# Attention of a hybrid mixer on one core: the two heads of a pair on the halves of the tensor engine's array

## The chip, the core and the metric

The kernel runs on one core of a Trainium2 chip. A core has a tensor engine (TensorE, PE in the views; PEld is its weight load), VectorE (DVE), ScalarE (ACT), GpSimd (POOL) and SyncE (SP), which work from queues of their own and wait for each other by semaphores. SBUF holds operands in 128 partitions, PSUM takes the matmuls' results in banks of 512 f32 columns. A matmul keeps one operand in the array (the stationary one, loaded ahead) and streams the other through it (the moving one). The metric is the device time of one execution in microseconds (us), less is better.

## What is computed

Two layers over 512 tokens of width 1024. Each layer projects the tokens, runs three mixers side by side (dilated attention with 8 heads of 64, retention, gated linear attention), multiplies by gates and an output matrix, and adds a feed forward with a short convolution; layer norms follow both. The change is in the attention, whose three dilated branches the reference computes and then merges:

```
scores = jnp.einsum('bhrnqd,bhrnkd->bhrnqk', qb, kk).astype(jnp.float32) * (d ** -0.5)
...
p = jnp.exp(scores - m[..., None])
l = p.sum(-1)
o = jnp.einsum('bhrnqk,bhrnkd->bhrnqd', p, vv) / l[..., None]
...
ya = merge_heads(head_norm(dilated_attention(qa, ka, va)))
```

The kernel takes the three branches at once: with a common maximum they are one softmax in which a key counts as often as branches see it (constant `mult`; `neg` masks the others). Head norm makes the common denominator drop out but for its epsilon, so the sums of values are normed as they are, with a term from the denominators (`ll`).

## The kernel before, in words

Every large product is made of leading and remaining parts, three passes each in fp32r (`mm3`, L202 to L205): lead x lead, lead x rest, rest x lead. Weights are loaded by SyncE's queue in tiles of 512 KB (`weight_tile`, L180), ScalarE rounds the leading part (L189), VectorE subtracts it (L190). Plain f32 products run as two passes each in the records. A transpose is a matmul with the identity (L277).

Attention (L573 to L677): for each of two groups of four heads, `project_heads` (L574) projects, rotates and transposes queries and keys: a block holds two heads, one in partitions 0 to 63, the other in 64 to 127. Values are projected once (`vv`, L663). The group has two pairs of heads (u = 0, 1), so a layer has four pairs and the kernel eight. For a pair:

- `scores` (L591), once for each head. Query tile i (128 tokens) meets the keys 0 to (i+1)*128, at least 256 columns, in three groups: tile 3, tile 2, tiles 0 and 1. The operands lie in 64 partitions, so the matmul uses the half of the array's rows in which its head lies. Each group takes one PSUM bank (`bank()`, four in all) and one page of SBUF (tag "pg", nine in all). VectorE masks, scales and finds the maximum (L607), ScalarE takes the exponential (L610), VectorE multiplies by `mult` and sums (L611).
- `weighted` (L616): for each head and each group of key tiles ((0,), (1, 3), (2,)) the numerators are transposed, 128 x 128 at a time, into a bank, ScalarE copies them to a page (L636), and `products` (L622) multiplies. There a 128 x 128 block of transposed numerators is the stationary operand and 64 columns of values move (L626): 10 matmuls for each head, all of a pair into one bank, tokens in the partitions. The transposes of a group come ahead of the products of the one before it.
- `finish` (L643): ScalarE squares the sums (L323), VectorE reduces them (L325), takes a reciprocal root (L304 to L308) and scales (L331). `finish_rows` (L648) transposes the pair's block after the next pair's scores, or, for the last pair, in the middle of the output product.

The order of the instructions is not written out by hand: a scheduler takes, for each engine, the ready instruction of the lowest number, with numbers set by `at(...)`. In a layer: pairs of the first group 6000 and 6400, values 7000, second group's heads 8000, its pairs 9000 and 9400, gates 9200, output product 20000. So while a pair waits for its softmax, TensorE's queue has projections. The order is fixed when the kernel is built; at run time each engine takes its queue in order.

Two other places use halves of the array and are not changed: L499 (states of the gated linear attention) multiplies 64 partitions by 64 partitions, one half of the rows for each value of c, into two banks; L555 writes 64 partitions of one bank with 64 stationary columns, then the other 64 with other operands.

Of the kernel before, what the change touches and what calls it, by code (L numbers as in the profile page):

```python
# [13 lines left out]
AF = mybir.ActivationFunctionType  # L14
ALU = mybir.AluOpType
# [25 lines left out]
def weight_chunks():  # L41
    """One layer's weights: name -> tiles of (rows, columns), in the order of their use."""
    w = {}
# [30 lines left out]
def weight_offsets():  # L74
    """(layer, name) -> tiles of (offset in the packed weights, rows, columns per row)."""
    at, out = 0, {}
    for l in range(DEPTH):
        for name, tiles in weight_chunks().items():
            out[l, name] = []
            for ks, c in tiles:  # L80
                out[l, name].append((at, len(ks), width(c)))
                at += P * len(ks) * width(c)
    return out
# [57 lines left out]
def hymba(ctx: ExitStack, tc: tile.TileContext, x, xt, wpk, prm, wal, lnv, cst, out):  # L141
# [38 lines left out]
    def weight_tile(l, name, i, lo_engine, raw=None):  # L180
        """A tile of weights: for each of its row blocks the leading and the remaining part."""
        o, nk, w = offsets[l, name][i]
# [28 lines left out]

# [1 line left out]
    c_sb = cp.tile([P, NCONST], F32, tag="cst", name="cst")  # L213
# [9 lines left out]
    def load_xt(t, raw, loads=1, parts=1):  # L223
        """A tile of tokens, transposed, in two parts: loaded at once or in pieces, and taken apart in pieces."""
        pieces = lambda a: a.rearrange("p (k t) -> p k t", k=KD)
# [18 lines left out]
    def start():  # L244
        """The first chunk of weights and the tokens, the first to be used ahead of the others. Products of zeros
        bring the tensor engine's clock up while they are loaded."""
        idle = page("yrg")
# [39 lines left out]
    def rope(ps, nh, dim, cname, t, a):  # L287
        """Rotates nh heads of dim from PSUM into a page."""
        half = dim // 2
# [11 lines left out]
    def rsqrt(v, n, tag):  # L301
        """v ** -0.5: an estimate from the exponent, and two Newton steps."""
        r, t = small(n, tag), small(n, tag)
        V.tensor_scalar(r.bitcast(I32), v.bitcast(I32), -0.5, 0x5F376908, op0=ALU.mult, op1=ALU.add)  # L304
        for c in (1.5008789, 1.5000006):
            V.tensor_mul(t, r, r)
            V.scalar_tensor_tensor(out=t, in0=t, scalar=-0.5, in1=v, op0=ALU.mult, op1=ALU.mult)
            V.scalar_tensor_tensor(out=r, in0=t, scalar=c, in1=r, op0=ALU.add, op1=ALU.mult)  # L308
        return r

    def centred(ps, out, tag):
        """Values less their mean over each head, so that the heads' outputs have mean zero."""
        p3 = ps.rearrange("p (g d) -> p g d", d=64)
# [6 lines left out]
    def normed(ps, more, scale, tag, small_tag):  # L320
        """Eight groups of 64 with mean zero, over the root of (their sum of squares + more)."""
        sq = page(tag)
# [12 lines left out]
    def to_rows(ps, scale, tag):  # L335
        """A block of the mixer's output, transposed, times its scale, as two parts."""
        h = page(tag, 512, F32R)
# [5 lines left out]
    def norm_rows(t, gb, last_layer):  # L343
        """Layer norm of token tile t, and out of the chip after the last layer."""
        mv = small(2, "s_ln")
# [18 lines left out]
    def to_columns():  # L364
        """The first of the normalized token tiles that wait for it, transposed, in two parts."""
        if pending:
# [16 lines left out]
    def token_gemm(rows, kt, tail, done, between=None):  # L383
        """Four token tiles of a product of rows[k] (stationary) and kt[k]; done(ps, t) takes each."""
        n = len(kt)
# [19 lines left out]
    for l in range(DEPTH):  # L405
# [4 lines left out]
        base = l * 1000000  # L410
# [1 line left out]
        at(base + 1000)  # L412
# [33 lines left out]
        at(base + 2500)  # L446
        # log sigmoid, its sums within chunks, and their exponentials
        la = page("yrg")
# [24 lines left out]
        bm128 = bmask.unsqueeze(2).to_broadcast([P, HR, P])  # L473
# [1 line left out]
        at(base + 3000)  # L475
# [12 lines left out]
        at(base + 4000)  # L488
        # states of the gated linear attention before each chunk
        gstate = [None] * 9  # L490
        for t2 in range(2):
# [13 lines left out]
            for u in range(4 if t2 == 0 else 3):  # L505
# [5 lines left out]
                gstate[i + 1] = s_  # L511
        # retention and gated linear attention, one token tile after another
        ynat = []
# [58 lines left out]

# [1 line left out]
        def project_heads(g):  # L574
            """Queries and keys of four heads, rotated and transposed, in two parts: blocks of two heads."""
            qk = x4("qk", F32R)
# [13 lines left out]

        def scores(qk, low, u, hh, l3):  # L591
            """Softmax's numerators of one head of pair u in a group, by query tile; sums into l3."""
            hs = slice(hh * 64, hh * 64 + 64)
            probs = [None] * NT
            nmx = small(4, "s_at")
            for group in ((3,), (2,), (0, 1)):
                sc, pr, o = bank(), page(), 0
                for i in group:
                    n, m = (i + 1) * P, max(256, (i + 1) * P)
                    ts = slice(i * P, (i + 1) * P)  # L600
                    mm3(sc[:, o:o + m], qk[hs, u, ts], low[u][hs, ts], qk[hs, 2 + u, 0:m], low[2 + u][hs, 0:m], True, True)
                    probs[i] = (sc[:, o:o + n], pr[:, o:o + n])
                    o += m
                for i in group:
                    s_, p_ = probs[i]
                    m0 = (3 - i) * P
                    V.tensor_tensor_reduce(out=p_, in0=s_, in1=C("neg")[:, m0:], op0=ALU.add, op1=ALU.min,  # L607
                                           scale=-0.125, scalar=3e38, accum_out=nmx[:, i:i + 1])
                    with tc.issue_after(tables.ins):
                        A.activation(out=p_, in_=p_, func=AF.Exp, scale=-1.0, bias=nmx[:, i:i + 1])  # L610
                    V.tensor_tensor_reduce(out=p_, in0=p_, in1=C("mult")[:, m0:], op0=ALU.mult, op1=ALU.add,  # L611
                                           scale=1.0, scalar=0.0, accum_out=l3[:, i, hh:hh + 1])
                    probs[i] = (s_, p_)
            return [p_ for _, p_ in probs]

        def weighted(pr, c0, o4):  # L616
            """The two heads' sums of values, weighted, into o4: a group of key tiles is transposed ahead of the
            products of the one before it."""
            groups = [(hh, js) for hh in range(2) for js in ((0,), (1, 3), (2,))]
            ready = []  # L620

            def products(hh, js, pt):  # L622
                o = 0
                for j in js:
                    for i in range(j, NT):
                        mmul(o4[:, i, hh, :], pt[:, o:o + P], vv[:, j, c0 + hh * 64:c0 + hh * 64 + 64],  # L626
                             start=(hh == 0 and j == 0 and i == 0), stop=(hh == 1 and js == groups[-1][1] and i == NT - 1))
                        o += P

            for hh, js in groups:  # L630
                bk, pt, o = bank(), page(), 0
                for j in js:
                    for i in range(j, NT):
                        transpose(bk[:, o:o + P], pr[hh][i][:, j * P:(j + 1) * P])
                        o += P
                A.copy(pt[:, :o], bk[:, :o])  # L636
                ready.append((hh, js, pt))
                if len(ready) > 1:
                    products(*ready.pop(0))
            for r in ready:  # L640
                products(*r)

# [15 lines left out]
        for g in range(2):  # L658
# [8 lines left out]
            for u in range(2):  # L667
# [3 lines left out]
                l3 = ll.rearrange("p (i h) -> p i h", h=2)  # L671
                pr = [scores(qk, low, u, 0, l3)]
                finish_rows()
                pr.append(scores(qk, low, u, 1, l3))
                o = bank()
                o4 = o.rearrange("p (i h d) -> p i h d", i=4, h=2)
                weighted(pr, p2 * P, o4)  # L677
                finish(o, ll, p2)

# [1 line left out]
        at(base + 9200)  # L681
# [13 lines left out]

# [1 line left out]
        stats = [sp.tile([P, 12], F32, tag="stats", name=nm("st"), bufs=8) for _ in range(NT)]  # L697
# [23 lines left out]

# [1 line left out]
        def conv(ps, c):  # L723
# [100 lines left out]
```

## Time and profile before

| | |
|---|---|
| time, median of 3 runs | 1265.61 us (1265.24 to 1268.29) |
| span of the profiled execution, first to last instruction | 1262.7 us |
| instructions | 15680 |
| TensorE busy | 1246.5 us, 99% |
| VectorE busy | 786.7 us, 62% |
| ScalarE busy | 448.0 us, 35% |
| DMA moved | 116.05 MB, mean 92 GB/s |

The profile gives the profiled execution's own time as its span of 1262.7 us; the timed runs contain also what lies before the first and after the last instruction. A matmul's duration runs from its issue to the end of its way through the array, and the next one begins before that, so prices of TensorE's work are read from start to start. A busy share says that an engine had something under way, not that it was at its peak.

### The profile page before, as it was taken

The numbers are of one execution on the slowest core, as the hardware profiler recorded it, in microseconds if no ns is written. First come the engines' busy times: TensorE is split into PE (matmuls) and PEld (weight loads), VectorE is DVE, ScalarE is ACT, GpSimd is POOL, SyncE is SP. The second block draws the span as 40 slices with busy tenths as digits, with TensorE's granted clock in tenths as the row PEclk, the third lists the DMA queues.
The fourth block names the chain that finished last, engine by engine and source line by source line (L and its number), as shares of the span: only waits on it lengthen the run. The fifth ranks groups of instructions, "written<-read, shape, count | busy, mean of one in ns | idle before, by whom it ended". The sixth has DMA issues, their size and how long they took to land.

```text
span 1262.7 us, 15680 instructions
## 1 busy us (share of the span) xinstructions
PE 1246.5 (99%) x6180; PEld 1036.1 (82%) x6180; DVE 786.7 (62%) x1519; ACT 448.0 (35%) x621; POOL 16.6 (1%) x26
## 2 busy tenths in 40 slices
PE   9999999999999999999999999999999999999997
PEld 7777888898888888888887778888988888888885
DVE  5676676587664356664767757767776633566646
ACT  5413344225442134442142134451444422444410
POOL 0010000000000000000000000000000000000000
PEclk9999999999999999999999999999999999999999
DMA  8302322223233233232242013222233322333221
GB/s 298 123 18 67 100 68 73 95 67 117 90 95 109 92 100 89 95 100 76 64 131 84 2 66 100 68 100 67 84 117 100 100 75 92 117 100 100 92 75 67
DMA packets 33401, 116.05 MB, mean 92 GB/s; under 512 B 3728, under 2 KB 4144, under 8 KB 33200
## 3 DMA queue, kind: packets, MB, share of 16 engines
q1 hardware_dynamic: 32176, 110.85, 27.1%
q0 software_dynamic: 1152, 4.19, 1.0%
q8 instruction: 49, 0.80, 0.3%
q14 instruction: 24, 0.20, 0.0%
HBM read 112.93 MB, written 2.10 MB: 91 GB/s over the span
## 4 chain that ended last, share of the span: by engine, by line
PE 94%; DVE 2%; DMA 2%; ACT 1%; issue 0%; SPq 0%; DVEq 0%; ACTq 0%
PE acc L203 25%; PE acc L204 25%; PE acc L205 25%; PE bk L626 3%; PE bk L277 3%; PE side L204 2%; PE side L205 2%; PE side L203 2%; DMA raw<-in_wpk 2%; PE bk L203 1%; DVE wlo L190 1%; PE bk L204 1%; PE bk L205 1%; PE side L277 1%; ACT whi L189 1%; PE bk L529 1%
## 5 line engine op out<-in xcount | busy, mean ns | idle before, releaser
L190 DVE TENSOR_TENSOR wlo<-raw,whi 128x1024 fp32r<-128x1024 f32 (+2 forms) x201 | 240.1, 1196 | 230.0 <-ACT whi L189 228.5
L189 ACT CAST whi<-raw 128x1024 fp32r<-128x1024 f32 (+2 forms) x201 | 206.2, 1026 | 352.1 <-PE side L205 133.8
L204 PE MATMUL acc<-xtl,whi 128*128 128x512 f32 (+1 forms) x768 | 288.7, 376 | 0.0
L205 PE MATMUL acc<-xth,wlo 128*128 128x512 f32 (+1 forms) x768 | 288.6, 376 | 0.0
L203 PE MATMUL acc<-xth,whi 128*128 128x512 f32 (+1 forms) x768 | 288.5, 377 | 0.0
L203 PEld LDWEIGHTS acc<-xth,whi 128*128 128x128 f32 x768 | 144.2, 188 | 27.8 <-issue 1.5
L204 PEld LDWEIGHTS acc<-xtl,whi 128*128 128x128 f32 x768 | 144.5, 188 | 26.5 <-DVE xtl L375 0.4
L205 PEld LDWEIGHTS acc<-xth,wlo 128*128 128x128 f32 x768 | 144.5, 188 | 26.0
L205 PE MATMUL acc<-whi,xtl 128*128 128x512 f32 (+1 forms) x384 | 147.0, 383 | 0.0
L204 PE MATMUL acc<-wlo,xth 128*128 128x512 f32 (+1 forms) x384 | 146.0, 380 | 0.8 <-DVE wlo L190 0.8
L203 PE MATMUL acc<-whi,xth 128*128 128x512 f32 (+1 forms) x384 | 146.3, 381 | 0.0
L203 PE MATMUL acc<-whi,yt 128*128 128x512 f32 x238 | 93.2, 392 | 0.0
L205 PE MATMUL acc<-whi,yt 128*128 128x512 f32 x238 | 92.9, 390 | 0.0
L204 PE MATMUL acc<-wlo,yt 128*128 128x512 f32 x238 | 92.7, 389 | 0.0
L204 PEld LDWEIGHTS acc<-wlo,xth 128*128 128x128 f32 x384 | 72.2, 188 | 14.8 <-DVE wlo L190 1.3
L727 DVE SCALAR_TENSOR_TENSOR pg<-acc,prm,pg 128x511 f32<-128x511 f32 x86 | 64.2, 747 | 32.0 <-ACT pg L726 31.9
L205 PEld LDWEIGHTS acc<-whi,xtl 128*128 128x128 f32 x384 | 72.1, 188 | 13.9 <-issue 2.2
L203 PEld LDWEIGHTS acc<-whi,xth 128*128 128x128 f32 x384 | 72.2, 188 | 12.9 <-issue 1.4
L726 ACT ACTIVATE pg<-acc,prm 128x512 f32<-128x512 f32 x86 | 66.9, 778 | 26.6 <-PE acc L205 26.6
L728 DVE SCALAR_TENSOR_TENSOR pg<-acc,prm,pg 128x510 f32<-128x510 f32 x86 | 64.4, 749 | 3.0
L379 DVE SCALAR_TENSOR_TENSOR x<-x,acc 128x512 f32<-128x512 f32 x38 | 26.1, 687 | 61.5 <-PE acc L205 61.5
L203 PE MATMUL acc<-whi,yrg 128*128 128x512 f32 x138 | 54.8, 397 | 0.0
(175 smaller groups left out, 1582.6 us busy)
## 6 DMA issues: line engine op xcount, KB each, us to landing
raw<-in_wpk SPq DMA_DIRECT2D x188, 512.0 KB, 3.6
gb<-in_lnv POOLq DMA_DIRECT2D x8, 512.0 KB, 4.7
x<-in_x SPq DMA_DIRECT2D x4, 512.0 KB, 5.8
raw<-in_wpk SPq DMA_DIRECT2D x8, 256.0 KB, 2.8
out<-x SPq DMA_DIRECT2D x8, 256.0 KB, 2.0
raw<-in_wpk SPq DMA_DIRECT2D x4, 408.0 KB, 4.1
xraw<-in_xt SPq DMA_DIRECT2D x3, 512.0 KB, 7.1
cst<-in_cst SPq DMA_DIRECT2D x1, 1222.0 KB, 9.0
```

The source lines that it names most:

```text
L189: nc.scalar.copy(hi, raw)
L190: lo_engine.tensor_sub(lo, raw, hi.bitcast(F32))
L203: nc.tensor.matmul(ps, ah, bh, start=first, stop=False)
L204: nc.tensor.matmul(ps, ah, bl, start=False, stop=False)
L205: nc.tensor.matmul(ps, al, bh, start=False, stop=last)
L277: nc.tensor.transpose(dst, src, ident)
L379: V.scalar_tensor_tensor(out=xr, in0=xr, scalar=scale, in1=ps, op0=ALU.mult, op1=ALU.add)
L529: mmul(sc, kT, qbd, start=True, stop=True)
L626: mmul(o4[:, i, hh, :], pt[:, o:o + P], vv[:, j, c0 + hh * 64:c0 + hh * 64 + 64], start=(hh == 0 and j == 0 and i == 0), stop=(hh == 1 and ...
L726: A.activation(out=u, in_=ps, func=AF.Identity, scale=w(2), bias=w(3))
L727: V.scalar_tensor_tensor(out=u[:, 1:], in0=ps[:, :S - 1], scalar=w(1), in1=u[:, 1:], op0=ALU.mult, op1=ALU.add)
L728: V.scalar_tensor_tensor(out=u[:, 2:], in0=ps[:, :S - 2], scalar=w(0), in1=u[:, 2:], op0=ALU.mult, op1=ALU.add)
```

## The change

`scores` takes both heads of a pair in one call. For each group it has two banks and two pages, and for each query tile the three passes alternate between the heads: head 0 (rows 0 to 63 of the array), head 1 (rows 64 to 127), and again. The softmax's instructions are the same, in the order group by group and in it head by head. The tile of maxima has 8 columns.

`weighted` turns the products round. The transposes and copies are the same, but group by group with both heads in each. The stationary operand is now 64 columns of values, and the transposed numerators of all query tiles that see the key tile move (512, 384, 256 or 128 columns). The two heads write the two halves of the partitions of one bank `oT`, which holds the transposed sums. ScalarE copies it to a page, and four transposes bring it into the bank `o` with tokens in the partitions, as `finish` wants it. Matmuls of products: 8 for a pair, 20 before. Transposes: 24 for a pair without `finish_rows`, 20 before. The rest of the diff removes comments and docstrings.

```
-        def scores(qk, low, u, hh, l3):
+        def scores(qk, low, u, l3):
...
             for group in ((3,), (2,), (0, 1)):
-                sc, pr, o = bank(), page(), 0
+                scs, prs, o = [bank(), bank()], [page(), page()], 0
                 for i in group:
                     n, m = (i + 1) * P, max(256, (i + 1) * P)
                     ts = slice(i * P, (i + 1) * P)
-                    mm3(sc[:, o:o + m], qk[hs, u, ts], low[u][hs, ts], qk[hs, 2 + u, 0:m], low[2 + u][hs, 0:m], True, True)
-                    probs[i] = (sc[:, o:o + n], pr[:, o:o + n])
+                    for step in range(3):
+                        for hh in range(2):
+                            hs = slice(hh * 64, hh * 64 + 64)
+                            q_ = (low[u][hs, ts] if step == 2 else qk[hs, u, ts])
+                            k_ = (low[2 + u][hs, 0:m] if step == 1 else qk[hs, 2 + u, 0:m])
+                            mmul(scs[hh][:, o:o + m], q_, k_, start=step == 0, stop=step == 2)
...
-        def weighted(pr, c0, o4):
+        def weighted(pr, c0):
...
-            groups = [(hh, js) for hh in range(2) for js in ((0,), (1, 3), (2,))]
+            groups = ((0,), (1, 3), (2,))
+            oT = bank()
             ready = []
 
-            def products(hh, js, pt):
+            def products(js, pts):
                 o = 0
                 for j in js:
-                    for i in range(j, NT):
-                        mmul(o4[:, i, hh, :], pt[:, o:o + P], vv[:, j, c0 + hh * 64:c0 + hh * 64 + 64],
-                             start=(hh == 0 and j == 0 and i == 0), stop=(hh == 1 and js == groups[-1][1] and i == NT - 1))
-                        o += P
...
+                    n = (NT - j) * P
+                    for hh in range(2):
+                        mmul(oT[hh * 64:hh * 64 + 64, j * P:], vv[:, j, c0 + hh * 64:c0 + hh * 64 + 64],
+                             pts[hh][:, o:o + n], start=j == 0, stop=js == groups[-1])
+                    o += n
+
+            for js in groups:
+                pts = []
+                for hh in range(2):
+                    bk, pt, o = bank(), page(), 0
+                    for j in js:
+                        for i in range(j, NT):
+                            transpose(bk[:, o:o + P], pr[hh][i][:, j * P:(j + 1) * P])
+                            o += P
+                    A.copy(pt[:, :o], bk[:, :o])
+                    pts.append(pt)
+                ready.append((js, pts))
                 if len(ready) > 1:
                     products(*ready.pop(0))
-            for r in ready:
-                products(*r)
+            products(*ready.pop(0))
+            ot = page()
+            A.copy(ot, oT)
+            o = bank()
+            for i in range(NT):
+                transpose(o[:, i * P:(i + 1) * P], ot[:, i * P:(i + 1) * P])
+            return o
...
-                pr = [scores(qk, low, u, 0, l3)]
+                pr = scores(qk, low, u, l3)
                 finish_rows()
-                pr.append(scores(qk, low, u, 1, l3))
-                o = bank()
-                o4 = o.rearrange("p (i h d) -> p i h d", i=4, h=2)
-                weighted(pr, p2 * P, o4)
+                o = weighted(pr, p2 * P)
                 finish(o, ll, p2)
```

## Rows read from the trace of the kernel before

**Rows 1.** The page: span, busy time by engine, chain that ended last.

```profile
span 1262.7 us, 15680 instructions
...
PE 1246.5 (99%) x6180; PEld 1036.1 (82%) x6180; DVE 786.7 (62%) x1519; ACT 448.0 (35%) x621; POOL 16.6 (1%) x26
...
PE 94%; DVE 2%; DMA 2%; ACT 1%; issue 0%; SPq 0%; DVEq 0%; ACTq 0%
```

**Rows 2.** Busy time in the two attention stretches: us, engines (instructions), TensorE clock, DMA.

```profile
104.00:231.00 127.00, 125.51 (x715) 105.46 (x714) 82.34 (x246) 52.84 (x92) 2.30 (x4) 1.00 0.25 80
...
729.00:856.00 127.00, 125.56 (x715) 105.50 (x715) 82.57 (x247) 53.20 (x92) 2.16 (x4) 1.00 0.25 80
```

**Rows 3.** Groups of TensorE by shape, xcount | busy us, mean ns: products, first score pass.

```profile
L626 PE MATMUL bk<-v,pg 128*128 128x64 f32 x320 | 40.6, 272 | 0.1
...
L203 PE MATMUL bk<-qk 64*128 64x512 f32 x16 | 7.9, 495 | 2.6 <-ACT qk L586 2.4
```

**Rows 4.** Timeline of TensorE (start us, duration us): transposes and one head's scores.

```profile
117.99 0.39 PE L203 MATMUL acc<-whi,xth 128*128 128x512 f32 x1
...
119.05 1.48 PE L277 MATMUL bk<-cst,pg 128*128 128x128 f32 x12
120.55 0.49 PE L203 MATMUL bk<-qk 64*128 64x512 f32 x1
...
121.12 0.39 PE L205 MATMUL bk<-qk,yrg 64*128 64x512 f32 x1
121.35 0.34 PE L203 MATMUL bk<-qk 64*128 64x384 f32 x1
121.53 0.34 PE L204 MATMUL bk<-yrg,qk 64*128 64x384 f32 x1
...
121.89 0.28 PE L203 MATMUL bk<-qk 64*128 64x256 f32 x1
...
122.12 0.28 PE L205 MATMUL bk<-qk,yrg 64*128 64x256 f32 x1
...
122.69 0.50 PE L204 MATMUL acc<-wlo,xth 128*128 128x512 f32 x1
```

**Rows 5.** The same view: a run of products and the matmul behind it.

```profile
137.39 3.01 PE L626 MATMUL bk<-v,pg 128*128 128x64 f32 x26
140.21 0.48 PE L205 MATMUL acc<-whi,xtl 128*128 128x512 f32 x1
```

**Rows 6.** The same view: L499, two halves of the rows, and what follows.

```profile
55.66 1.99 PE L499 MATMUL bk<-yt,yrg 64*128 64x256 f32 x14
57.59 0.33 PE L277 MATMUL bk<-cst,pg 128*128 128x128 f32 x1
```

**Rows 7.** The same view: L555, two halves of the columns, and what follows.

```profile
67.15 0.43 PE L555 MATMUL bk<-cst 128*64 128x256 f32 x1
67.16 0.43 PE L555 MATMUL bk<-yt,yrg 128*64 128x256 f32 x1
67.42 0.38 PE L555 MATMUL bk<-cst 128*64 128x256 f32 x1
67.42 0.38 PE L555 MATMUL bk<-yt,yrg 128*64 128x256 f32 x1
67.73 0.44 PE L277 MATMUL bk<-cst,pg 128*128 128x128 f32 x2
```

**Rows 8.** The same view: two f32 passes of 512 columns, and what follows.

```profile
79.18 1.02 PE L535 MATMUL bk<-pg,yrg 128*128 128x512 f32 x2
80.04 0.59 PE L542 MATMUL bk<-pg,pg 128*128 128x256 f32 x2
```

**Rows 9.** Line L636, copies of transposed numerators: duration ns, min/median/max.

```profile
L636 ACT COPY pg<-bk x48: 363/576/590, 115.4 to 847.7; 128x512 f32<-128x512 f32 x32, 128x256 f32<-128x256 f32 x16
```

**Rows 10.** Timeline of VectorE: norm of the first layer's last pair, [idle before <-releaser].

```profile
225.44 0.69 DVE L325 TENSOR_REDUCE s_at<-pg 128x8 f32<-128x512 f32 x1 [4.22 <-ACT pg L323]
```

**Rows 11.** Timeline of TensorE: that pair's block transposed.

```profile
230.62 0.60 PE L277 MATMUL bk<-cst,pg 128*128 128x128 f32 x4
```

More of the change, by code (lines that the diff above doesn't have):

```diff
@@ L589, in project_heads @@
             return qk, low
-        def scores(qk, low, u, hh, l3):
-            hs = slice(hh * 64, hh * 64 + 64)
-            probs = [None] * NT
-            nmx = small(4, "s_at")
+        def scores(qk, low, u, l3):
+            probs = [[None] * NT, [None] * NT]
+            nmx = small(8, "s_at")
             for group in ((3,), (2,), (0, 1)):
-                sc, pr, o = bank(), page(), 0
+                scs, prs, o = [bank(), bank()], [page(), page()], 0
                 for i in group:
@@ L600, in scores @@
                     ts = slice(i * P, (i + 1) * P)
-                    mm3(sc[:, o:o + m], qk[hs, u, ts], low[u][hs, ts], qk[hs, 2 + u, 0:m], low[2 + u][hs, 0:m], True, True)
-                    probs[i] = (sc[:, o:o + n], pr[:, o:o + n])
-                    o += m
[L604 to L613, printed above, removed]
@@ L614, in scores @@
-            return [p_ for _, p_ in probs]
-        def weighted(pr, c0, o4):
-            groups = [(hh, js) for hh in range(2) for js in ((0,), (1, 3), (2,))]
+                    for step in range(3):
[4 more added lines that the diff above has]
+                            mmul(scs[hh][:, o:o + m], q_, k_, start=step == 0, stop=step == 2)
@@ new lines, in scores @@
+                    for hh in range(2):
+                        probs[hh][i] = (scs[hh][:, o:o + n], prs[hh][:, o:o + n])
+                    o += m
+                for hh in range(2):
+                    for i in group:
+                        s_, p_ = probs[hh][i]
+                        m0 = (3 - i) * P
+                        mx = nmx[:, 4 * hh + i:4 * hh + i + 1]
+                        V.tensor_tensor_reduce(out=p_, in0=s_, in1=C("neg")[:, m0:], op0=ALU.add, op1=ALU.min,
+                                               scale=-0.125, scalar=3e38, accum_out=mx)
+                        with tc.issue_after(tables.ins):
+                            A.activation(out=p_, in_=p_, func=AF.Exp, scale=-1.0, bias=mx)
+                        V.tensor_tensor_reduce(out=p_, in0=p_, in1=C("mult")[:, m0:], op0=ALU.mult, op1=ALU.add,
+                                               scale=1.0, scalar=0.0, accum_out=l3[:, i, hh:hh + 1])
+                        probs[hh][i] = p_
@@ L620, in weighted @@
+            return probs
+        def weighted(pr, c0):
+            groups = ((0,), (1, 3), (2,))
+            oT = bank()
             ready = []
-            def products(hh, js, pt):
+            def products(js, pts):
                 o = 0
                 for j in js:
-                    for i in range(j, NT):
-                        mmul(o4[:, i, hh, :], pt[:, o:o + P], vv[:, j, c0 + hh * 64:c0 + hh * 64 + 64],
-                             start=(hh == 0 and j == 0 and i == 0), stop=(hh == 1 and js == groups[-1][1] and i == NT - 1))
-                        o += P
@@ L630, in weighted @@
[L630 to L637, printed above, removed]
+                    n = (NT - j) * P
+                    for hh in range(2):
+                        mmul(oT[hh * 64:hh * 64 + 64, j * P:], vv[:, j, c0 + hh * 64:c0 + hh * 64 + 64],
+                             pts[hh][:, o:o + n], start=j == 0, stop=js == groups[-1])
@@ new lines, in products @@
+                    o += n
+            for js in groups:
+                pts = []
+                for hh in range(2):
+                    bk, pt, o = bank(), page(), 0
[6 more added lines that the diff above has]
+                ready.append((js, pts))
```

## The prediction

> **What bounds the kernel now.** I read the page first: its busy line and the chain of waits. TensorE is busy for 1246.5 of 1262.7 us and 94% of the chain that ended last is TensorE's; DMA and VectorE have 2% each [rows 1]. Busy alone says little where matmuls overlap, so I looked next at the stretches of the two layers that hold the attention [rows 2]: of 127 us, TensorE 125.5, VectorE 82, ScalarE 53, at the full granted clock (1.00, 2.4 GHz). Between the attention's pieces the queue holds projections, so a wait of the softmax is covered, and a microsecond of TensorE's stream that goes is a microsecond of the kernel, as long as that cover lasts. Then the groups of TensorE by shape [rows 3] say what the change touches: 320 passes of products with 64 columns (two passes for each fp32 instruction: 20 instructions in each of 8 pairs of heads), the scores (16 heads, 12 passes each), and transposes. Last, the timeline gives prices, start to start, because the durations overlap.
>
> **What a piece costs now.** One head's scores: 0.23 us for a 512-column pass (121.12 to 121.35), 0.18 for 384, 0.115 for 256 (two in 121.89 to 122.12). A head has 3, 3 and 6 of these: 0.69 + 0.54 + 0.69 = 1.92 us. The run stands on the engine for 2.14 (120.55 to 122.69), and the full-array matmul behind it takes 0.50 us where its like takes 0.39 [rows 4]. So going to half rows and back costs 0.22 + 0.11, say 0.3 us: I call this a visit. Sixteen heads: 16 x (1.92 + 0.3) = 35.5 us. Products: 26 passes in 140.21 - 137.39 = 2.82 us [rows 5], 0.1085 each, 34.7 us for 320. That is as much as a whole 128-column transpose next door (12 in 1.50 us [rows 4]), though only 64 columns stream: here the operand that is loaded sets the pace.
>
> **Do halves run together?** The trace of before has one case of each kind. Row halves: the 14 passes of L499 (256 columns, K of 64, the two halves of the keys) stand for 57.59 - 55.66 = 1.93 us [rows 6]. At full array two fp32 passes of 512 columns take 0.86 us [rows 8], so 256 columns take 0.215 and 14 in a row would be 3.01. Most of them overlap. Column halves: the two instructions of L555 start 0.01 us apart, and their second passes again together, 0.27 later; all four are through in 67.73 - 67.15 = 0.58 us [rows 7], against 0.86 one after another. So both kinds overlap, with different moving data in each half.
>
> **Scores.** The change lets two heads, in two row halves, follow each other pass by pass into two banks. The stream of a pair falls from 2 x 1.92 to 1.92. Four banks hold two of the three groups; the third waits until VectorE has read the first, so I take two visits for a pair: 8 x (1.92 + 0.6) = 20.2 us, against 35.5: **-15.3**. Bounds: one visit 2.4 better, three 2.4 worse.
>
> **Products.** Values are loaded (64 columns), the transposed numerators stream: 512 + 384 + 256 + 128 = 1280 columns a head, two passes, at 0.43 us per 512 [rows 8]: 2.15 us, both heads together. They come in three groups between transposes, and each group is a visit to column halves. In L555 the visit costs 0.58 - 0.43 = 0.15 inside [rows 7] and something at its edge; I take the 0.3 of the scores. 8 x (2.15 + 0.9) = 24.4, against 34.7: **-10.3**. The bounds of a visit, 0.15 and 0.45, are 3.6 us either way.
>
> **Transposes back.** Four more in each pair, 32 x 0.125 [rows 4] = **+4.0**.
>
> **The copy and the longer chain.** ScalarE gets one more 512-column copy for each pair, 0.58 us (the median of the like [rows 9]): 4.6 us for an engine that is busy 53 of 127; VectorE's work is the same. The copies do not bound. What they do is lengthen the way from the last product to the normed sums by a copy and four transposes, about 1.1 us. In six pairs projections cover that. In the last pair of each layer the cover is the first half of the output product: VectorE waits 4.22 us, begins the norm at 225.44 [rows 10], and the block is transposed at 230.62 [rows 11], with TensorE full meanwhile. After the change TensorE has some 2.7 us less of its own in this pair and comes to that point earlier, while the softmax on VectorE takes as long as before. So I put the wait between 0 and 1.1 us for each of eight pairs (8.8), and take 2.3 for each layer: **+4.6**. No DMA, no other queue, no weight is moved.
>
> **The sum.** -15.3 - 10.3 + 4.0 + 4.6 = -17.0 us. The profiled span is 1262.7; the median of the three runs shown is 1265.6, that is 2.9 us for what lies around it, which stays. Span after: 1245.7; time: **1248.6 us**. The own range of this case is 1243 to 1255 (visits and wait at their ends).
>
> A table of the Trainium skill speaks for less. "TensorE: Matmul & The Clock Gate", Part 3, measured 2.38 times for three column tiles and 3.07 for four row tiles, not 3 and 4. An estimate from it, at 0.79 and 0.77 of the ideal: the pair's scores gain a factor of 1.53 and the products 1.59, which is 4.7 + 4.4 us less gain, 1257.7 us. The rows of L499 and L555 stand at 3.01 / 1.93 = 1.56 and 0.86 / 0.58 = 1.48 with their visits counted in [rows 6, 7]. I count visits apart, so I keep my sum.
>
> **Rivals.** (a) Products overlap only partly. For: the second head's transposed page is copied some 0.6 us after the first's [rows 9], other work may slip between, and an instruction has two passes; if only the first head's second pass and the second's first meet, three pass times of four are left: 8 x (3 x 1.075 + 0.9) = 33.0. The gain of 10.3 shrinks to 1.7: 1257.2 us. Against: L555 shows both passes together [rows 7]. 0.20. The same page of the Trainium skill, Part 3, has matmuls start and end strictly in program order; taken to the letter it gives this case, and L555's starts do not agree.
>
> (b) The stage is no longer bound by TensorE: with scores of both heads taken at once (six pages, four banks) the next pair begins later, VectorE's chain shows. VectorE has 82 of 127 us [rows 2], 70% of the 118 that would be left; it does not bind as a sum, only where fillers run out. Price: half of the gain of 21.6 before waits is given back, 1254.8. 0.12.
>
> (c) Scores do not overlap: no row shows two one-pass (fp32r) matmuls in two halves, which ask for twice the columns per microsecond of L499. Without the 15.3 the time is 1263.9, no change. 0.06.
>
> (d) **Slower**: in the queue the two heads' products stand apart, each behind its own copy with a projection between. Then nothing overlaps and each of 64 instructions is a visit: 8 x 4.3 + 64 x 0.3 = 53.6 us, 18.9 over before; with the other terms 18.9 - 15.3 + 4.0 + 4.6 = +12.2: 1277.8. Every pair of instructions that stays together gives back half its stream (0.54) and a visit (0.3), so it needs under 15 of the 32 together to be slower at all. The two follow each other in program order and are ready some 0.6 us apart, so 0.06.
>
> **How the numbers follow.** My case 0.56, (a) 0.20, (b) 0.12, (c) 0.06, (d) 0.06. The first three are faster by more than 0.3% (3.8 us, about what a measurement here tells from no change): 0.88; (c) is within it, 0.06; (d) slower, 0.06. The range of 1242 to 1260 us takes in my case and (a) and (b) and leaves (c) and (d) outside.
>
> **What would show it.** In the changed trace: score passes of two heads starting within 0.02 us of each other, about 0.23 us to the next 512-column pair; 128 passes of products (64 instructions) instead of 320, 512 columns in 0.43 us for both halves; 32 transposes and 8 copies more; the two attention stretches each 8 to 9 us shorter, the rest equal. Wrong if passes of two heads start a full pass apart, if TensorE shows idle time with ScalarE or VectorE as releaser inside the stretch, or if the stretches shrink and the feed forward grows.

## The result, and the profile after

The changed kernel takes **1256.19 us** (median of 4 runs, 1255.33 to 1257.98), the kernel before 1265.42 in the same runs: a ratio of 0.9917 [0.9896, 0.9937], 9.2 us less. The forecast was 1248.6 with a range of 1242 to 1260. Sign and range hold; 17 us were promised, and a little over half came.

The page of the changed kernel, the lines that answer to [rows 1]:

```profile
span 1253.6 us, 15361 instructions
...
PE 1233.8 (98%) x6020; PEld 1004.1 (80%) x6020; DVE 786.7 (63%) x1519; ACT 453.1 (36%) x629; POOL 15.9 (1%) x26
...
PE 90%; DMA 4%; DVE 3%; ACT 2%; issue 0%; SPq 0%; DVEq 0%; ACTq 0%
```

VectorE's work is the same to a tenth, ScalarE has its eight copies more (5.1 us), TensorE 160 matmuls less: 192 of the products gone, 32 transposes more. TensorE's share of the chain of waits falls from 94% to 90%, and DMA, VectorE and ScalarE take the difference. The two attention stretches, same columns as [rows 2]:

```profile
104.00:231.00 127.00, 123.55 (x654) 92.81 (x653) 85.46 (x251) 57.44 (x97) 2.31 (x4) 1.00 0.27 85
729.00:856.00 127.00, 124.78 (x655) 94.43 (x655) 84.73 (x249) 55.15 (x94) 2.17 (x4) 1.00 0.25 80
```

The clock is as it was (1.00, the 2.4 GHz level). From the first score pass to the first residual of the output product each layer's stretch went from 127.1 and 126.9 us to 122.7 and 122.4; these 8.9 us are all of the change but 0.2, so nothing was lost in the feed forward. The forecast had 8 to 9 us for each stretch; it is 4.4 and 4.5.

To see what the 9 us are made of I summed TensorE's time start to start over the whole trace, by kind of pass, a pause counted to what stands before it ("rest" is everything else, the projections above all). Differences to the kernel before in us, from the profiled executions (a later section adds the experiments):

| | scores | products | transposes of pages | rest | span |
|---|---|---|---|---|---|
| before, in all | 33.1 | 34.4 | 22.0 | 1173.2 | 1262.7 |
| forecast | -15.3 | -10.3 | +4.0 | +4.6 | -17.0 |
| changed | -5.8 | -12.2 | +3.6 | +5.3 | -9.1 |

The products and the transposes came as forecast. The scores did not. The rest came near its forecast, but by other things than the one forecast: of its 5.3 us, 2.1 are pauses, and 2.3 are projection passes of 512 columns that now stand next to one of the attention's pieces (104 of them, 86 before; these take 0.31 us from start to start, the others 0.23). Where the scores fell short is in the timeline of the third pair of layer 0 (start us, duration us, [idle before <-releaser]):

```profile
173.87 0.68 PE L606 MATMUL bk<-qk 64*128 64x512 f32 x4
174.40 0.50 PE L606 MATMUL bk<-yrg,qk 64*128 64x512 f32 x2
174.74 0.40 PE L606 MATMUL bk<-qk,yrg 64*128 64x512 f32 x2
174.98 0.33 PE L606 MATMUL bk<-yrg,qk 64*128 64x384 f32 x2
175.15 0.34 PE L606 MATMUL bk<-qk,yrg 64*128 64x384 f32 x2
175.42 0.50 PE L203 MATMUL acc<-whi,xth 128*128 128x512 f32 x1
175.75 0.40 PE L204 MATMUL acc<-wlo,xth 128*128 128x512 f32 x1
176.83 0.38 PE L606 MATMUL bk<-qk 64*128 64x256 f32 x1 [0.68 <-DVE s_at L615]
177.06 0.28 PE L606 MATMUL bk<-yrg,qk 64*128 64x256 f32 x1
177.17 0.28 PE L606 MATMUL bk<-qk,yrg 64*128 64x256 f32 x1
177.29 0.28 PE L606 MATMUL bk<-qk 64*128 64x256 f32 x1
177.41 0.28 PE L606 MATMUL bk<-yrg,qk 64*128 64x256 f32 x1
177.44 0.38 PE L606 MATMUL bk<-qk 64*128 64x256 f32 x1
177.66 0.28 PE L606 MATMUL bk<-yrg,qk 64*128 64x256 f32 x1
177.67 0.39 PE L606 MATMUL bk<-qk,yrg 64*128 64x256 f32 x2
...
178.34 0.33 PE L277 MATMUL bk<-cst,pg 128*128 128x128 f32 x1
```

The first two groups do what was forecast: the passes stand in pairs (x2, two heads), their starts 3 to 4 ns apart in the trace, and a 512-column pair inside a run is followed after 0.24 us (174.74 to 174.98), the time of one pass alone before [rows 4]. (The first pair of a run takes 0.34, as a first pass alone did; of the 12 pairs inside runs, two take 0.34 as well, one of them that of 174.40.) The third group, tiles 0 and 1, begins after a pause for VectorE and then goes mostly one pass at a time: 12 passes in 1.51 us (176.83 to 178.34), where six pairs of 0.115 would be 0.69. In the whole trace all 24 pairs of 512 columns overlap (starts within 0.02 us), 16 of 24 with 384, but only 14 of 48 with 256. VectorE at the same time:

```profile
174.94 1.22 DVE L190 TENSOR_TENSOR wlo<-raw,whi 128x1024 fp32r<-128x1024 f32 x1 [0.40 <-ACT whi L189]
176.09 0.68 DVE L615 CUSTOM_DVE_ANT_0 pg<-bk,cst 128x512 f32<-128x512 f32 x1
176.69 0.08 DVE L615 DVE_READ_ACCUMULATOR2_ANT s_at<- 128x1 f32 x1
176.69 0.69 DVE L615 CUSTOM_DVE_ANT_0 pg<-bk,cst 128x512 f32<-128x512 f32 x1
```

The four banks hold tile 3 and tile 2 of both heads. The third group's first pass (176.83) needs the first bank back, which VectorE reads at 176.09, behind a weight conversion of 1.22 us, and its other head needs the second, read from 176.69. The queue's order fits that lag: five passes of head 0, for which the first bank is enough, stand ahead of the first of head 1 (177.44), and at run time the queue goes in order. A rival for the pause itself is the weight conversion: without it VectorE could have begun some 0.9 us sooner, as the first scores were through at 175.14. No run moved it.

TensorE's waits over the whole kernel, us in total, times, longest:

```profile
PE bk L606 <- DVE s_at L615: 2.6, 4, 0.7
PE bk L606 <- ACT qk L586: 1.7, 2, 0.9
PE side L277 <- DVE yt L704: 1.1, 2, 0.6
PE bk L277 <- DVE pg L331: 0.5, 1, 0.5
```

Before, the same view had 2.4 for `qk` (it shows in [rows 3]) and none of the other three. So new waits of 4.2 us stand in the way: for a bank (L615, in the second and third pair of each layer), for the gated values' transposes in the fourth pair (L704), and 0.5 in the norm of the last pair, where I had put 4.6. All pauses of TensorE together are 5.6 us before and 9.2 after, 0.5 of the difference ahead of 10 us, where nothing was changed.

### The profile page after: what moved, and what is told of

Same layout as the page of the kernel before. It is cut to its first block, busy times and chain, and to the rows that moved or that the text cites. A ratio compares the mean times of both kernels' runs of the same rounds, so it can differ in the third digit from the quotient of the medians.

```text
span 1253.6 us, 15361 instructions
## 1 busy us (share of the span) xinstructions
PE 1233.8 (98%) x6020; PEld 1004.1 (80%) x6020; DVE 786.7 (63%) x1519; ACT 453.1 (36%) x629; POOL 15.9 (1%) x26
## 4 chain that ended last, share of the span: by engine, by line
PE 90%; DMA 4%; DVE 3%; ACT 2%; issue 0%; SPq 0%; DVEq 0%; ACTq 0%
PE acc L205 25%; PE acc L203 25%; PE acc L204 25%; DMA raw<-in_wpk 4%; PE bk L277 3%; PE side L204 2%; PE side L203 2%; PE side L205 2%; DVE wlo L190 2%; ACT whi L189 2%; PE bk L636 2%; PE bk L606 1%; PE side L277 1%; PE bk L529 1%; PE bk L535 1%; PE bk L549 1%
```

## Experiments

All twelve are kernels of their own, with the kernel before timed on the same chip. Medians, ratios to the kernel before with 95% intervals:

| run | what | us | ratio |
|---|---|---|---|
| e1_products_alone | scores as before | 1256.38 | 0.9923 [0.9900, 0.9946] |
| e2_scores_alone | products as before | 1261.32 | 0.9966 [0.9950, 0.9982] |
| e3_paired_scores | alternation forced | 1255.67 | 0.9918 [0.9896, 0.9941] |
| e4_split_copies | one head's copies on VectorE | 1260.83 | 0.9952 [0.9934, 0.9970] |
| e5_no_back | sums not transposed back | 1251.86 | 0.9892 [0.9876, 0.9908] |
| e6_five_banks | side's bank in the pool | 1273.62 | 1.0058 [1.0040, 1.0075] |
| e7_one_pool | all eight banks in one pool | 1397.28 | 1.1041 [1.1015, 1.1068] |
| e8_one_pool_products_alone | the same, scores as before | 1411.39 | 1.1153 [1.1134, 1.1172] |
| e9_one_run | a pair's products in one run | 1254.99 | 0.9916 [0.9900, 0.9931] |
| e10_one_run_products_alone | the same, scores as before | 1258.06 | 0.9940 [0.9924, 0.9956] |
| e11_one_run_order | e9, smaller group first | **1249.35** | 0.9858 [0.9835, 0.9882] |
| e12_one_run_order_paired | e11, alternation forced | 1250.27 | 0.9866 [0.9845, 0.9888] |

Against what was expected of them: e1, e2 and e5 came out just under the range that fits them best, e4, e6, e7 and e8 slower than any range given, e9 between its two, and e11 over 2 us better than its own.

And the account of TensorE's time, as above, differences to the kernel before:

| run | scores | products | transposes of pages | rest | span |
|---|---|---|---|---|---|
| changed | -5.8 | -12.2 | +3.6 | +5.3 | -9.1 |
| e2 | -6.5 | +0.4 | -0.9 | +3.6 | -3.4 |
| e3 | -7.5 | -12.4 | +3.9 | +6.7 | -9.3 |
| e4 | -5.3 | -9.8 | +3.6 | +5.6 | -5.9 |
| e5 | -4.4 | -12.2 | +0.8 | +3.5 | -12.3 |
| e9 | -6.0 | -15.4 | +3.8 | +6.2 | -11.4 |
| e10 | +0.4 | -15.4 | +5.2 | +4.1 | -5.7 |
| e11 | -8.4 | -15.4 | +3.9 | +4.9 | -15.0 |
| e12 | -10.4 | -15.4 | +4.4 | +7.0 | -14.4 |

### Each half of the change alone

The diffs here are against the changed kernel unless another is named. e1 takes `scores` back:

```
-        def scores(qk, low, u, l3):
+        def scores(qk, low, u, hh, l3):
...
-                pr = scores(qk, low, u, l3)
+                pr = [scores(qk, low, u, 0, l3)]
                 finish_rows()
+                pr.append(scores(qk, low, u, 1, l3))
```

> The new products and the transposes back, with the scores of before (one head after the other). If the parts add up: the products' stretch falls from 34.4 us to about 22.3 as in the changed kernel, transposes and copies cost 3.6 to 4, so 6.5 to 8.5 us less than before: 1257 to 1259 us. If instead the gain of the change hangs on both parts together (banks and pages shared in another way), this part alone is within 3 us of before.

e2 takes `weighted` back:

```
-        def weighted(pr, c0):
+        def weighted(pr, c0, o4):
...
-                o = weighted(pr, p2 * P)
+                o = bank()
+                o4 = o.rearrange("p (i h d) -> p i h d", i=4, h=2)
+                weighted(pr, p2 * P, o4)
```

> The new scores with the products of before (transposed numerators stationary, 64 columns of values moving, no transposing back). If the scores are the part that fell short: their stretch falls from 33.1 us to about 27 and waits ahead of them take some of it, so 1 to 4 us less than before, 1261.5 to 1264.5. If the scores did give their 15 us and something else took it back: 1250 to 1253.

The products alone give 9.1 us, as much as the whole change (1256.38 and 1256.19); the scores alone give 4.2. Together that would be 13.3, and it is 9.2; the missing 4.1 us are about as large as the three intervals allow, so that the halves stand in each other's way is likely but not shown. (The profiled execution of e1 has a granted clock of 0.97 in the first stretch, so it is left out of the account; so are e6 to e8, whose clock is lower too. In layer 1, where e1's clock is 1.00, the stretch from first score to residual is 126.9 us before, 122.9 in e1, 125.2 in e2 and 122.4 with both.) The new scores take less time in each case, -5.8 and -6.5, and the rest takes much of it back, +5.3 and +3.6. e1 shows no pause of TensorE for a score's bank and none for L704; in the changed kernel these two are the 3.7 us seen above, in e2 2.6, so they come with the new scores.

### Is it the order of the passes?

If the lone passes of the third group are the loss, forcing the alternation gets it back. e3 lets each pass be issued only behind the one before it:

```
+                last = None
...
-                            mmul(scs[hh][:, o:o + m], q_, k_, start=step == 0, stop=step == 2)
+                            with tc.issue_after(last.ins) if last else ExitStack():
+                                last = mmul(scs[hh][:, o:o + m], q_, k_, start=step == 0, stop=step == 2)
```

> The changed kernel, with every score pass of a group kept behind the pass ahead of it in the program, so that the two heads alternate in the queue in every group. Theory (order): in the changed kernel 68 of 96 passes of 256 columns and 16 of 48 of 384 run alone because the queue holds one head's passes of a group and then the other's; alternating takes 34 x 0.117 + 8 x 0.18 = 5.4 us out of the stream, less a visit to half rows more in some pairs: 1251 to 1253 us. Rival (waits): TensorE waits for VectorE to free banks, and passes that alternate wait for the later of two banks: 1255.5 to 1258.

40 of 48 pairs of 256 columns now overlap, and the time is 1255.67, the changed kernel's within its spread. The scores lost 1.7 us of stream more and the rest took 1.4 back. The third pair again, now of e3:

```profile
174.58 0.35 PE L608 MATMUL bk<-qk,yrg 64*128 64x384 f32 x2
174.86 0.50 PE L203 MATMUL acc<-whi,xth 128*128 128x512 f32 x1
175.20 0.40 PE L204 MATMUL acc<-wlo,xth 128*128 128x512 f32 x1
176.36 0.38 PE L608 MATMUL bk<-qk 64*128 64x256 f32 x1 [0.77 <-DVE s_at L617]
176.68 0.50 PE L205 MATMUL acc<-whi,xtl 128*128 128x512 f32 x1
177.01 0.40 PE L203 MATMUL acc<-whi,xth 128*128 128x512 f32 x1
177.34 0.38 PE L608 MATMUL bk<-qk 64*128 64x256 f32 x1
177.34 0.50 PE L608 MATMUL bk<-yrg,qk 64*128 64x256 f32 x2
177.57 0.39 PE L608 MATMUL bk<-qk,yrg 64*128 64x256 f32 x2
...
178.24 0.66 PE L277 MATMUL bk<-cst,pg 128*128 128x128 f32 x4
```

The passes run in twos from 177.34, but the group still waits at 176.36, its first pass goes alone, two projection passes follow, and the array is taken to halves and back a second time. The group ends 0.1 us earlier than in the changed kernel, having begun 0.5 earlier. In the whole trace the scores stand in 28 runs (22 in the changed kernel), the bank's wait is 2.9 us (2.6), and all pauses are 9.5 (9.2). So what the pairs saved was paid at the ends of six more runs, hardly in waits: 116 projection passes now stand next to one of the attention's pieces, 104 in the changed kernel, and these are the 1.4 us of the rest. The order by itself is not the loss. That a run breaks because the second bank is not yet back can be read from the rows, one pass at 176.36 and the others from 177.34; e3 does not separate it.

### Who frees the banks, and how many there are

e4 takes work from ScalarE, so that the two heads' transposed pages are copied at once, and gives it to VectorE:

```
-                    A.copy(pt[:, :o], bk[:, :o])
+                    (A.copy if hh == 0 else V.tensor_copy)(pt[:, :o], bk[:, :o])
```

> The changed kernel, with the copy of head 1's transposed numerators on VectorE in place of ScalarE. In the changed kernel the two heads' 512-column products start 0.15 to 0.36 us apart, one copy after the other. If that lag is what the products still lose, 0.3 x 8 = 2.4 us less: 1253.5 to 1254.5. If VectorE's softmax stands in the way of the copies, 0 to 3 us more: 1256 to 1259.

It is 4.6 us slower than the changed kernel. Its window of layer 0 has VectorE at 90.75 of 127 us, 5.3 more, and the weight load of the products now waits for that copy:

```profile
PEld bk L636 <- DVE pg L648: 2.1, 8, 0.4
```

The two engines' copies in e4, duration ns min/median/max:

```profile
L648 ACT COPY pg<-bk x24: 372/582/589, 116.2 to 840.9; 128x512 f32<-128x512 f32 x16, 128x256 f32<-128x256 f32 x8
L648 DVE COPY pg<-bk x24: 424/682/693, 117.8 to 841.1; 128x512 f32<-128x512 f32 x16, 128x256 f32<-128x256 f32 x8
```

The second head's page came later, not sooner: the heads' 512-column products start 0.42 to 0.48 us apart (0.15 to 0.36 in the changed kernel). VectorE needs 0.68 us for a copy where ScalarE needs 0.58, and in the fourth pair of layer 0, where the lag grew most (0.48 from 0.15), its copies come behind a weight conversion. Products cost 2.4 us more than in the changed kernel, in 20 runs for 18. So VectorE has over a quarter of its time free in this stretch, and the copies still come later there.

e6 gives the pool a fifth bank, that of the projections' side tiles; e7 makes one pool of all eight, e8 is its control with the old scores:

```
-    ps_side = ctx.enter_context(tc.tile_pool(name="ps_side", bufs=1, space=bass.MemoryType.PSUM))
-    ps_sm = ctx.enter_context(tc.tile_pool(name="ps_sm", bufs=4, space=bass.MemoryType.PSUM))
+    ps_sm = ctx.enter_context(tc.tile_pool(name="ps_sm", bufs=5, space=bass.MemoryType.PSUM))
...
-        return ps_side.tile([P, 512], F32, tag="side", name=nm("side"))
+        return ps_sm.tile([P, 512], F32, tag="sm", name=nm("side"))
```

> The changed kernel with five small PSUM banks in place of four and one (the side tiles are drawn from the same five). Theory (banks): the scores' third group needs two banks that VectorE has still to read, so TensorE waits or runs it one head at a time; a fifth bank takes away one of the two waits: 1 to 3 us less, 1253 to 1255. Rival (the gain is spent elsewhere, in visits and in the softmax's pace): 1255.5 to 1257.

> The changed kernel with all eight PSUM banks in one pool (accumulators, side and small tiles), so that all six banks of a pair's scores can be had at once and the queue holds 24 alternating passes in one run. Theory (banks): scores at 8 x (1.94 + 0.3) = 17.9 us in place of 27.3 and waits of the scores gone (3 us): 8 to 12 us less, 1244 to 1248, unless other stages lose by the common pool. Rival (softmax's pace or visits): within 3 us of the changed kernel, 1253 to 1259.

> Control for the one pool: new products, scores of before (one head after the other), all eight banks in one pool. Theory (banks): these scores take one bank at a time, so the pool alone brings little: 1254 to 1258, and the kernel with new scores in one pool is 6 to 10 us faster than this. Rival: the pool itself helps, whatever the scores: this one gains as much as that one.

All three are slower than the kernel before, so they do not measure what a bank is worth to the scores alone: the other users lost theirs. They do show what a bank does to the pairs: of the 96 pairs of score passes 54 overlap in the changed kernel with its four banks, 66 in e6 with five (18 of 48 of 256 columns) and 90 in e7 with eight (all 48). In e6 TensorE waits 9.0 us for VectorE's sums of the softmax ahead of transposes, in e7 the projections' transposes wait for the rotation:

```profile
PE side L275 <- DVE rope L297: 33.6, 15, 2.3
```

In e7 the granted clock is lower too. The stretch from 104 to 231 us, columns as before, is not the same work as above, as its scores begin only at 149.6; TensorE is busy for 100.94 of the 127 us, at a mean clock of 0.85 of 2.4 GHz:

```profile
104.00:231.00 127.00, 100.94 (x456) 76.42 (x456) 62.29 (x175) 34.20 (x55) 1.25 (x2) 0.85 0.17 56
```

e7 is 14.1 us faster than e8, which differs from it in the scores alone. With four banks the same difference (changed kernel against e1) is 0.2 us. In the profiled executions it is 9.3, of which 3.4 and 3.2 lie in the two layers' attention stretches and 2.7 ahead of the first. So in these kernels the number of passes that overlap rises with the banks; what that is worth in time the runs do not settle.

### The way back, and the products in one run

e5 leaves out the copy of `oT` and its four transposes, so heads and tokens stay swapped in what is normed; it prices that step:

```
-            ot = page()
-            A.copy(ot, oT)
-            o = bank()
-            for i in range(NT):
-                transpose(o[:, i * P:(i + 1) * P], ot[:, i * P:(i + 1) * P])
-            return o
+            return oT
```

> The changed kernel without the copy of the transposed sums and without the four transposes back: the norm reads the transposed sums as they are, so the attention's outputs are arranged wrongly; everything else runs. This prices the new tail of a pair. If it costs what its matmuls stream, 32 x 0.11 = 3.5 us: 1252 to 1253. If the longer way to the norm also holds TensorE up in each pair (up to 1.1 us each, 8.8 us): 1244 to 1248. If it lies beside a wait anyway: 1255 to 1256.

4.3 us less than the changed kernel (3.2 in the profiled spans). Its transposes are 2.8 us less, its rest 1.8 less, its scores 1.4 more. So the way back costs about its stream: the longer chain to the norm, 4.6 in the forecast, hardly shows. The price is not quite clean, as a pair of e5 also takes one bank less; its wait for a bank is 0.6 us (2.6), that for `qk` 3.4 (1.7).

The second loss in the trace was a lag in the products. In the changed kernel the 512-column products of a pair do not start together, since the second head's page is copied after the first's; e9 leaves them all for one run behind the last transposes:

```
-                if len(ready) > 1:
-                    products(*ready.pop(0))
-            products(*ready.pop(0))
+            for r in ready:
+                products(*r)
```

> The changed kernel, with a pair's products all behind its last transposes, in one run in place of two or three. Theory (visits): one visit to column halves less in each pair (8 x 0.3 = 2.4 us) and no lag between the heads' 512-column products (8 x 0.15 to 0.36 = 1 to 3 us): 1251 to 1254 us. Rival (cover): the transposes now have no products between them and TensorE waits for ScalarE's copies, six in a row at 0.5 us: 1256 to 1261.

> The same with the scores of before, one head after the other. If products and scores do not add up because both draw on the same cover (projections between the pieces), this one is as fast as the one with new scores, within 1.5 us. If they add up once the products stand in one run, this one is 2 to 4 us slower than the one with new scores.

The first run of products, changed kernel:

```profile
118.82 1.38 PE L636 MATMUL bk<-pg,v 128*64 128x512 f32 x4
120.13 0.66 PE L277 MATMUL bk<-cst,pg 128*128 128x128 f32 x4
```

and e9:

```profile
118.46 1.08 PE L636 MATMUL bk<-pg,v 128*64 128x512 f32 x4
119.47 0.50 PE L203 MATMUL acc<-whi,xth 128*128 128x512 f32 x1
```

1.31 us against 1.01 to the next instruction; in e9 the two heads' passes start 6 to 8 ns apart, in the changed kernel up to 0.36 us. With 12 runs for 18 the products fall by another 3.2 us. Of this 2.3 is left in the span and 1.2 in the median, within the runs' spread: the wait for a bank rises from 2.6 to 3.3 us. e10, the same with the old scores, is 3.1 us slower than e9, so here the new scores give something.

### Giving the bank back sooner

If VectorE's first read decides, a smaller first group should free the bank sooner and find its pages sooner. e11 is e9 with the groups in another order, e12 the same with the passes chained as in e3:

```
-            for group in ((3,), (2,), (0, 1)):
+            for group in ((2,), (3,), (0, 1)):
```

> One run of products (as in e9) and the scores' groups in the order tile 2, tile 3, tiles 0 and 1. VectorE frees the first group's banks by two reads of 384 columns (0.55 us each) in place of 512 (0.69), and the passes of the second group are longer, so the third group should find its banks 0.3 + 0.15 us sooner in each pair. Theory (the third group waits for VectorE's reads): TensorE's waits on the banks, 3.3 us in e9, fall to under 2, and the time is 1 to 3 us below e9: 1252 to 1254. Rival (the wait only moves): 1254.5 to 1257.

> The same with the two heads kept in alternation as in e3. If with banks free sooner the alternation pays: 2 to 4 us below e9, 1251 to 1253, with under 30 score passes alone. If, as in e3, every pass saved comes back as a wait or a visit: equal to e11 within 1 us.

**1249.35 us**, 16 us below the kernel before and the best of the study. Layer 0's first pair in e11:

```profile
102.71 0.44 PE L606 MATMUL bk<-qk 64*128 64x384 f32 x2
...
103.20 0.34 PE L606 MATMUL bk<-qk,yrg 64*128 64x384 f32 x2
103.46 0.50 PE L203 MATMUL acc<-whi,xth 128*128 128x512 f32 x1
...
108.59 0.62 PE L606 MATMUL bk<-qk 64*128 64x512 f32 x4 [1.33 <-ACT qk L586]
109.05 0.29 PE L606 MATMUL bk<-yrg,qk 64*128 64x256 f32 x2
109.17 0.28 PE L606 MATMUL bk<-qk,yrg 64*128 64x256 f32 x2
```

and its wait for a bank:

```profile
PE bk L606 <- DVE s_at L615: 1.1, 2, 0.9
```

Tile 2 needs no key of the last token tile, so its scores run at 102.7, while the last tile is still being projected; by the time tile 3 comes, VectorE has emptied their banks, and here the third group finds two free and runs in twos beside it. Scores fall from 22 runs to 16; 24 of 48 pairs of 256 columns overlap (14 in e9) and all 24 of 384 (16), but only 16 of 24 of 512 (24). By the forecast's prices the runs are the larger part of the 2.4 us that the scores lose against e9: 6 x 0.3 = 1.8, and the pairs 10 x 0.115 + 8 x 0.18 - 8 x 0.23 = 0.75. The wait for a bank is a third of e9's, all pauses are 8.6 us (10.0). The attention begins sooner than in e9 (102.7 for 106.6; 719.5 for 726.1 in layer 1). Whether the sooner bank or the sooner start gives more was not separated. e12 gets two more us out of the scores' stream and gives them all back in the rest: chaining is worth nothing here either.

## Why the prediction was right, and where its sum failed

The range held; the sum missed by 7.6 us. The range of 1242 to 1260 was drawn wide enough for rivals (a) and (b). The case's own, 1243 to 1255, misses 1256.19, and its parts, two visits' bounds and a wait of 0 to 8.8, give 1238 to 1259 when all are taken at their ends. One of the forecast's own signs of being wrong came true as well: TensorE waits for VectorE inside the stretches.

**Right: the halves overlap.** Row halves with one-pass matmuls, the case that no row of before showed, take 0.24 us for a 512-column pair inside a run, about what one pass took: rival (c) is out. Column halves too, both passes of an fp32 instruction: rival (a) is out for 48 of the 64 pairs of passes, and the 16 of 512 columns overlap for half of their way. Rival (d) did not occur: no product stands apart from its pair.

**Right: the products.** -12.2 against -10.3, within the bounds of a visit. The sum had 24 visits and no lag; the trace has 18 runs, and 0.3 us of lag in each pair.

**Right: the transposes back**, +3.6 for +4.0.

**Failed: the scores' term**, -15.3, by the step "the stream of a pair falls from 2 x 1.92 to 1.92" with "two visits for a pair". Measured is -5.8, 9.5 us short. By the forecast's own prices 68 lone passes of 256 columns and 16 of 384 are 34 x 0.115 + 8 x 0.18 = 5.4 us more stream, and 22 runs instead of 16 are 6 x 0.3 = 1.8, of which the account puts a part, the slower matmul behind a run, elsewhere. Another 1.6 are pauses that the account counts to the scores, because a score pass stands before them (1.1 of it the wait for L704). These are at most 8.8 of the 9.5; the rest is not assigned. I had seen that "the third waits until VectorE has read the first", and priced it as a visit; but half of the passes are in that third group, and the two banks it needs come back one after the other, a read of 0.6 us apart.

**Near in size by luck: the wait.** +4.6 stood for the norm of the last pair in each layer. There it was 0.5 us. But waits of 3.7 us for VectorE appeared in the scores and beside them, where I had none. That the rest of the account is +5.3 does not bear the term out: 2.3 of it are slower projection passes at the edges of more pieces, which the sum did not have.

So the kernel went by a mixture of my case and rival (b), "six pages, four banks", at 1254.8. Rival (a)'s 1257.2 and the estimate of 1257.7 lie as near by number, but the products, where (a) had the loss, gained more than forecast. For (b)'s mechanism, that TensorE goes through its part faster than VectorE returns banks, speak the rows of the third pair, the waits that e1 lacks, and the overlap that rises with the banks in e6 and e7; that the sooner bank is what pays in e11 is argued, not shown. The Trainium skill has the rule: "TensorEngine Tiling (Array Packing)", under Performance Considerations, PSUM Bottleneck, says that tiling speeds up TensorE but not the emptying of PSUM. The 0.68 us before 176.83 agree. Its advice to empty with ScalarE and VectorE both is what the changed kernel does already (VectorE reads the scores, ScalarE copies); putting more of the copies on VectorE cost 4.6 us (e4).

## What to carry to other kernels

When two streams are made to run side by side, count the banks that both need at once and when each comes back; a pair that needs two banks runs as a pair only from the later one, and forcing the order of the passes gives nothing then (e3, e12). Price each half of such a change alone and together: here they gave 9.1, 4.2 and 9.2 us. Count also how often a change of shape breaks the stream: fewer runs paid in e9 and e11, more runs took back what e3 won. What paid most was to give the slow consumer a smaller piece first, one whose inputs are also ready early; which of the two counts more is open.

## What the runs showed that was not expected

- Two one-pass matmuls of 512 columns in two row halves take 0.24 us together, what one took, with starts 3 to 4 ns apart. "TensorE: Matmul & The Clock Gate" of the Trainium skill, Part 3, has that lag, but factors of 2.38 and 3.07 for three and four tiles; for two row halves these rows show almost no loss within a run, only at its ends.
- Two fp32 instructions in column halves start 7 ns apart and take their second passes together 0.48 us later (e9), so their passes are not taken one after the other. Such a pair of passes takes 0.48 us where one at full array takes 0.43 [rows 8].
- Products are cheaper in fewer, longer runs: six runs less and no lag are 3.2 us in e9, of which the lag is 8 x 0.3 = 2.4.
- Moving four banks' worth of separate pools into one cost 141 us (e7 against the changed kernel), more than scores, products and transposes took together before (89.5).
